# Storing h as hi and lo parts, loading them from GpSimd's queue, and S5 and linear attention without GpSimd arithmetic

## Chip, cores and metric

The kernel runs on one core of a Trainium2 chip. The metric is the device time of one execution in microseconds (us). An engine is called by its name in the profile: PE (TensorE matmuls), DVE (VectorE), ACT (ScalarE), POOL (GpSimd) and SP (SyncE, which begins most transfers).

## What is computed

One decoder layer on 2048 tokens of width 1024. A modulated RMSNorm gives h; one projection of h feeds three token mixers (gated linear attention, sparse attention over the best 256 keys, and the S5 state-space layer), whose outputs are joined by one projection; a mixture of 32 experts follows. Cut to what the change touches:

```
h = rms_norm(x, norm1_g) * (1 + sc1) + sh1
proj = h @ w_in                       # 2616 columns, split among the mixers
g = log_sigmoid(lr @ gate_w + gate_b) / GLA_TAU          # gates of linear attention
bcum = cumsum(g); q_dec = q * exp(bcum); k * exp(-bcum); k * exp(blast - bcum)
o = rms_norm(o, norm_g) * silu(r)                         # linear attention
_, _, h_re, h_im = associative_scan(combine, (a_re_t, a_im_t, x_re, x_im))   # S5
score = where(admissible, score, -inf); _, sel = top_k(score, 256)           # sparse attention
```

## The kernel before

h is kept in fp32 precision by writing each operand of a product as hi + lo, both rounded to a 32-bit form that PE multiplies faster; a product is then three matmuls (`mm3`, lines 162 to 164). Weights are split in `load_split` (ACT makes hi in line 176, DVE or POOL the rest in line 177).

**Sweep 1** (`prep`, `tok1`, `scores`, lines 308 to 411) goes over the tokens in 8 chunks of 256. It builds h transposed (`ht`), splits it into `xh` (DVE, line 333) and `xl` (POOL, line 334), stores `ht` to `hT_d` in DRAM by a transfer of SP (line 335), and projects the columns for the indexer and for `u`; the indexer's scores are accumulated on DVE (line 255).

**The later sweeps** (`sweep2`, line 445) need h again for the other columns: 2a (the `v` and `r` columns, 410 to 547 us in the profile), 2b (`gqk_d`, to about 684 us), 2c (the rest of `r` and `dv_d`, to about 775 us) and, later, DQ (`dqk_d`, about 1045 to 1245 us). Each has 8 chunks; for each chunk `load_h` (line 431) brings two tiles `xr` of 512 KB by SP (line 437), ACT makes hi from each (line 440) and POOL lo (line 441). `load_h` for the next chunk stands at the start of a chunk.

Between 420 and 775 us the sweeps are woven with the choice of the 256 keys: ten rounds of counting (`select`), in which ACT counts one part of the keys (line 805) and DVE another (line 808), then DVE joins the counts in some fifteen instructions of 14 numbers each (lines 812 to 836). DVE also computes the parameters of S5 (`params`) and the gates' sums (`gates`, lines 549 to 555, with a subtraction on POOL in line 552). `masks` (from line 844) follows: a penalty per block of keys (line 858 on DVE, line 859 on DVE or POOL) and a mask.

**S5 and linear attention** (775 to 1045 us): `s5_tables` (line 909) builds power tables for 6 groups at a time, three instructions per table, by `powers` (lines 929 to 934); `TGI` says which of the four tables POOL builds (0, 2 and 3; DVE builds the fourth). `s5_states` (line 1168) and `s5_outputs` (line 1202) use them, and linear attention (`gla_prep`, `gla_block`, `gla_tail`) is woven in; its last part runs beside DQ. At about 819 us all engines meet at a branch on a flag (line 1013).

A scheduler orders each engine's instructions when the program is built, from dependences and an own estimate of times; so a change in one place moves instructions in others. Each engine takes its instructions in that order, and a transfer on a queue waits behind those before it.

The instruction of line 441 that much of the prediction speaks of is this:

```
S.activation(xx[0][-1], xr, AF.Copy)
G.tensor_sub(xx[1][-1], xr, xx[0][-1].bitcast(F32))
```

Of the kernel before, what the change touches and what calls it, by code (L numbers as in the profile page):

```python
# [9 lines left out]
F32 = mybir.dt.float32  # L10
# [4 lines left out]
AF = mybir.ActivationFunctionType  # L15
# [5 lines left out]
P = 128  # L21
# [19 lines left out]
def body(tc, x, c, ada_w, ada_b, norm1_g, w_in, gla_gate_w, gla_gate_b, gla_norm_g, dsa_norm_g,  # L41
# [97 lines left out]


    C1 = 256
    hT_d = dr.tile([KD, P, T], F32, name="hT_d")
    u_d = dr.tile([T, 384], F32, name="u_d")
    v_d = dr.tile([T, 384], F32, name="v_d")
    r_d = dr.tile([T, 384], F32, name="r_d")
# [162 lines left out]
    def prep(ch):  # L308
# [16 lines left out]
        for k0 in range(0, KD, 4):  # L325
            ht = s1.tile([P, KD * P], F32, name="ht", tag="ht").rearrange("p (k c) -> p k c", c=C1)
            for k in range(k0, k0 + 4):
                pt = s1p.tile([P, 2, C1], F32, name="pt", tag="pt", bufs=2)[:, 0]
                for i in range(2):
                    TE.transpose(pt[:, i * P:(i + 1) * P], xs[i][:, k * P:(k + 1) * P], ident)  # L330
                S.activation(ht[:, k - k0], pt, AF.Identity, scale=gain[:, k:k + 1], bias=modc[:, 0, k:k + 1])
                yield
            V.tensor_copy(xh[:, k0:k0 + 4], ht)
            G.tensor_sub(xl[:, k0:k0 + 4], ht, xh[:, k0:k0 + 4].bitcast(F32))
            nc.sync.dma_start(hT_d[k0:k0 + 4, :, t0:t0 + C1].rearrange("k p t -> p k t"), ht)
        iqs = ts_.tile([P, 8, C1], F32R, name="iqs", bufs=2)
        st_[ch] = (xh, xl, iqs)
        for m in (2, 0, 1):
# [87 lines left out]

    SWA = 12
    SCO = list(range(2, NB))
    WB, PPB, PJB, XRB, XXB = 3, 3, 3, 4, 3

    def load_h(ch):

        t0 = ch * C1
        xx = [[], []]
        for k0 in range(0, KD, 4):
            xr = fp.tile([P, 4, C1], F32, name="xr", tag="xr", bufs=XRB)
            nc.sync.dma_start(xr, hT_d[k0:k0 + 4, :, t0:t0 + C1].rearrange("k p t -> p k t"))
            for j in range(2):
                xx[j].append(fp.tile([P, 4, C1], F32R, name=f"xx{j}", bufs=XXB))
            S.activation(xx[0][-1], xr, AF.Copy)  # L440
            G.tensor_sub(xx[1][-1], xr, xx[0][-1].bitcast(F32))  # L441
        return xx
    xx_ = {}

    def sweep2(job, last=False):
# [23 lines left out]
        for ch in range(T // C1):  # L469
            t0 = ch * C1  # L470
            xx = xx_.pop(ch)
            nx = (ch + 1) % (T // C1)
            if nx or not last:
                xx_[nx] = load_h(nx)
            if feat:
                ft = fp.tile([P, 4, C1], F32, name="ft", tag="xr", bufs=4)

                pps = [fpp.tile([P, 2, C1], F32, name="pp", bufs=PPB) for m in range(2)]
                for z in range(2):
                    for m in range(4):  # L480
                        for k in range(z * 4, z * 4 + 4):
                            mm3(pps[m // 2][:, m % 2], [w[:, k, m * P:(m + 1) * P] for w in w2],
                                (xx[0][z][:, k % 4], xx[1][z][:, k % 4]), k, KD - 1, -1 if m % 2 else 0,
                                skip_group_check=True)
                        if m % 2:
                            if z:
                                S.activation(ft[:, m - 1:m + 1], pps[m // 2], AF.Copy)  # L487
                            yield
                nc.sync.dma_start(job[1][:, :, t0:t0 + C1].rearrange("m p t -> p m t"), ft)
            else:  # L490
                N = sum(n for _, n, _, _ in job)
                pjs = [fpp.tile([P, 512], F32, name="pj", bufs=PJB)[:, :N] for i in range(2)]
                for z in range(2):
                    for i in range(2):
                        cs = slice(i * P, (i + 1) * P)
                        for k in range(z * 4, z * 4 + 4):
                            mm3(pjs[i], (xx[0][z][:, k % 4, cs], xx[1][z][:, k % 4, cs]),
                                (w2[0][:, k, :N], w2[1][:, k, :N]), k, KD - 1)
                        if z:
                            tok_store(job, ch * 2 + i, fp, pjs[i])  # L500
                        yield
# [18 lines left out]
    def gates():  # L520
        with tc.tile_pool(name="gg", bufs=1, side="right") as gg, \
# [15 lines left out]
            for t0 in range(0, T, H2):  # L537
                lr = gg.tile([16, H2], F32, name="lr")
                nc.sync.dma_start(lr, lr_d[:, t0:t0 + H2])
                for p_ in range(2):  # L540
                    ta = gg.tile([P, H2], F32, name="ta")
                    tm = gg.tile([P, H2], F32, name="tm")
                    for c0 in range(0, H2, CH):
                        cs = slice(c0, c0 + CH)
                        pg = ggp.tile([P, CH], F32, name="pg")
                        TE.matmul(pg, wg[:, 2 * p_:2 * p_ + 2].rearrange("r h d -> r (h d)"), lr[:, cs], start=True,
                                  stop=True)
                        S.activation(ta[:, cs], pg, AF.Abs, bias=gb2[:, p_:p_ + 1])
                        V.tensor_scalar(tm[:, cs], pg, gb2[:, p_:p_ + 1], 0.0, op0=OP.add, op1=OP.min)
                    S.activation(ta, ta, AF.Exp, scale=-1.0)  # L550
                    S.activation(ta, ta, AF.Ln, bias=1.0)
                    G.tensor_sub(tm, tm, ta)
                    for c0 in range(0, H2, CH):
                        cs = slice(c0, c0 + CH)
                        V.tensor_tensor_scan(ta[:, cs], rst, tm[:, cs], 0.0, op0=OP.mult, op1=OP.add)
                    nc.sync.dma_start(bc_d[p_, :, t0:t0 + H2], ta)
                    yield
# [338 lines left out]
    pnx = ExitStack()  # L896
    pn = pnx.enter_context(tc.tile_pool(name="pn", bufs=2, side="right"))
    MSK = [(masks(list(z), a_, i, pn), 2 * len(z)) for i, (z, a_, e, _) in enumerate(SELS)]
    RJ, TGI = (), (0, 2, 3)
    SPT, SPU, SPY, TGT, TGY = 1, 2, 1, 't', 'y'  # L900
    s5x = ExitStack()
    s5 = s5x.enter_context(tc.tile_pool(name="s5", bufs=2))
# [162 lines left out]
    def gla_prep(ch):  # L1065
# [13 lines left out]
        S.activation(o.enb, o.enb, AF.Exp, scale=-1.0 / 16.0)  # L1079
        o.qd, o.ki = o.gq[:, 0:2], o.gq[:, 2:4]  # L1080
        V.scalar_tensor_tensor(o.qd, o.qd, 48.0 ** -0.5, o.eb, op0=OP.mult, op1=OP.mult)
        G.tensor_mul(o.ki, o.ki, o.enb)
        G.tensor_mul(o.kd.rearrange("p m (n c) -> p m n c", c=64), o.ki.rearrange("p m (n c) -> p m n c", c=64),
                     o.eb[:, :, 63::64][:, :, :, None].to_broadcast([P, 2, 4, 64]))
        o.og = ga.tile([P, 2, 384], F32, name="og")
        o.ss = ga.tile([P, 2, 4], F32, name="ss")
# [2 lines left out]
    def gla_block(o, i):  # L1089
# [35 lines left out]
        sq = ga.tile([P, 384], F32, name="sq")  # L1125
        S.activation(sq, o.og[:, i], AF.Square)
        V.tensor_reduce(o.ss[:, i], sq.rearrange("p (h c) -> p h c", h=4), op=OP.add, axis=AX)
        G.tensor_mul(o.rt[:, i], o.rt[:, i], o.og[:, i])

    def gla_tail(o, ch):  # L1130
        t0 = ch * C1
# [32 lines left out]
    with tc.tile_pool(name="s5s", bufs=2) as s5s:  # L1164
# [3 lines left out]
        def s5_states(t):  # L1168
# [14 lines left out]
            for n in range(NS_):  # L1183
# [3 lines left out]
                V.tensor_mul(xa[:, n], px[:, 0], ct[:, g0 + n])  # L1187
                V.tensor_mul(xb[:, n], px[:, 1], st[:, g0 + n])
                yield
            G.tensor_add(xa, xa, xb)  # L1190
            for n in range(NS_):
                gg = gb * GB + g0 + n
                V.tensor_tensor_scan(gt[:, n], prm[:, 4, gg:gg + 1].to_broadcast([P, NCK]), xa[:, n], 0.0,
                                     op0=OP.mult, op1=OP.add)
            yield
            V.memset(p1[:, :, :, 0:1], 0.0)
            G.tensor_mul(p1[:, 0, :, 1:], gt[:, :, :NCK - 1], ct[:, ss_, :NCK - 1])
            V.scalar_tensor_tensor(p1[:, 1, :, 1:], gt[:, :, :NCK - 1], -1.0, st[:, ss_, :NCK - 1], op0=OP.mult,
                                   op1=OP.mult)
            yield  # L1200
# [970 lines left out]
```

## Time and profile before

| What | us |
|---|---|
| Runs: median of 3 (lowest to highest) | 2953.65 (2953.2 to 2962.46) |
| The profiled execution's own time | 2958.35 |
| Its span | 2956.3 |
| Mean granted clock of PE (share of full) | 0.883 |
| PE busy | 2390.8 (81%) |
| DVE busy | 2105.1 (71%) |
| ACT busy | 1345.6 (46%) |
| POOL busy | 1032.1 (35%) |

The profile is one execution; times in it are counted from its span's start. Busy time is summed per engine; what an engine waited for is inferred from its semaphores. Shares over the whole span say little here, since the stages have different limits; the stages named above are read one by one.

### The profile page before, as it was taken

How to read it: one execution, taken by the hardware profiler on the slowest of the kernel's cores; microseconds unless marked ns; L12 is line 12 of the kernel's file. 1: busy time of each engine (PE TensorE's matmuls, PEld its weight loads, DVE VectorE, ACT ScalarE, POOL GpSimd, SP SyncE). 2: the span in 40 equal slices, each digit the busy share in tenths (PEclk: the TensorE clock that was granted, in tenths of full speed). 3: DMA queues.
4: the chain of work that ended last, by engine and by line, in shares of the span. 5: the costliest groups of instructions: out<-in, count | busy, mean ns of one | idle time of the engine just before them, and what ended most of it. 6: DMA issues, size and time to landing. Idle time of an engine off the chain costs nothing. (4 is left out here: it accounts for less than half of the span.)

```text
span 2956.3 us, 38623 instructions
## 1 busy us (share of the span) xinstructions
PE 2390.8 (81%) x12563; PEld 1866.4 (63%) x12563; DVE 2105.1 (71%) x4742; ACT 1345.6 (46%) x2337; POOL 1032.1 (35%) x765
## 2 busy tenths in 40 slices
PE   4989877777568899948897999488877988889995
PEld 3766645776546767736675778476655566656673
DVE  6478867999988864547787565677766777667774
ACT  2568867574122244446665222155433444444442
POOL 2221133436645332155543345304322333222321
PEclk9999967888776879958998899688988999989998
DMA  7222254433331244244322543397777888778882
GB/s 217 86 92 85 80 201 155 113 136 124 107 114 46 71 153 126 84 140 121 100 80 86 174 143 130 91 288 212 250 225 228 261 269 262 243 252 267 277 259 82
DMA packets 372280, 474.93 MB, mean 161 GB/s; under 512 B 85924, under 2 KB 272452, under 8 KB 371814
## 3 DMA queue, kind: packets, MB, share of 16 engines
q1 hardware_dynamic: 334501, 421.83, 44.6%
q0 software_dynamic: 37568, 50.56, 6.2%
q8 instruction: 100, 1.64, 0.2%
q14 instruction: 111, 0.90, 0.1%
HBM read 385.75 MB, written 112.23 MB: 168 GB/s over the span
## 5 line engine op out<-in xcount | busy, mean ns | idle before, releaser
L1921 DVE TENSOR_TENSOR wl<-wraw,wh 128x1024 fp32r<-128x1024 f32 x272 | 329.1, 1220 | 162.5 <-ACT wh L1920 156.3
L1920 ACT ACTIVATE wh<-wraw 128x1024 fp32r<-128x1024 f32 x272 | 286.2, 1054 | 296.7 <-PE pd L164 107.8
L1970 PE MATMUL pg<-xT,wh 128*128 128x352 f32 (+10 forms) x1152 | 325.4, 362 | 12.0 <-DVE xT L1902 6.7
L1944 PE MATMUL pg<-wraw,xT 128*120 128x512 f32 (+9 forms) x448 | 225.0, 663 | 82.0 <-DVE ga__21999 L1977 12.9
L1972 PE MATMUL pg<-xT,wl 128*128 128x176 f32 (+10 forms) x1152 | 283.7, 246 | 1.5 <-DVE wl L1921 1.5
L441 POOL TENSOR_TENSOR xx<-xr,xx 128x1024 fp32r<-128x1024 f32 x64 | 162.9, 2546 | 273.2 <-ACT xx L440 261.1
L1970 PEld LDWEIGHTS pg<-xT,wh 128*128 128x128 f32 x1152 | 224.1, 195 | 17.2 <-DVE xT L1902 7.9
L1972 PEld LDWEIGHTS pg<-xT,wl 128*128 128x128 f32 x1152 | 227.3, 197 | 2.5 <-DVE wl L1921 2.0
L1944 PEld LDWEIGHTS pg<-wraw,xT 128*120 128x120 f32 (+9 forms) x448 | 85.8, 196 | 212.3 <-issue 115.5
L255 DVE SCALAR_TENSOR_TENSOR sb<-rl,iws,sb 128x1024 f32<-128x1024 f32 (+7 forms) x154 | 186.6, 1211 | 33.3 <-ACT rl L254 24.9
L2018 POOL DMA_INDIRECT yp_d<-y,ix x50 | 94.4, 1887 | 311.0 <-DVE y L2015 173.5
L162 PE MATMUL pd<-wh,hid 128*104 128x512 f32 (+17 forms) x400 | 163.5, 409 | 23.8 <-ACT hid L1954 12.3
L162 PE MATMUL pp<-xx,w 128*128 128x256 f32 x512 | 155.1, 303 | 20.1 <-ACT ft L487 10.0
L254 ACT ACTIVATE rl<-pi,iwa 128x1024 f32<-128x1024 f32 (+7 forms) x176 | 157.2, 910 | 30.5 <-DVE sb L255 25.9
L163 PE MATMUL pd<-wl,hid 128*104 128x512 f32 (+17 forms) x400 | 159.5, 399 | 0.0
L164 PE MATMUL pd<-wh,hid 128*104 128x512 f32 (+17 forms) x400 | 158.7, 402 | 0.0
L163 PE MATMUL pp<-xx,w 128*128 128x256 f32 x512 | 152.7, 299 | 3.1 <-POOL xx L441 3.1
L164 PE MATMUL pp<-xx,w 128*128 128x256 f32 x512 | 152.0, 298 | 2.0 <-DVE w L177 1.2
L251 PE MATMUL pi<-iks,iqs 128*128 128x512 f32 (+3 forms) x304 | 110.9, 448 | 32.1 <-ACT rl L254 31.2
L162 PE MATMUL pj<-w,xx 128*128 128x512 f32 (+1 forms) x256 | 100.2, 393 | 40.7 <-DVE ot L208 19.2
L1538 DVE CUSTOM_DVE_ANT_0 pr<-ps,mk 128x512 f32<-128x512 f32 (+3 forms) x160 | 94.2, 605 | 49.9 <-PE ps L1537 28.2
L2005 POOL DMA_INDIRECT part<-yp_d,ix x50 | 68.6, 1373 | 163.2 <-DMA yp_d<-y,ix 154.2
(1076 smaller groups left out, 6975.9 us busy)
## 6 DMA issues: line engine op xcount, KB each, us to landing
wraw<-in_exp_w_gate_dram SPq DMA_DIRECT2D x128, 512.0 KB
wraw<-in_exp_w_up_dram SPq DMA_DIRECT2D x128, 512.0 KB
wraw<-in_exp_w_down_dram SPq DMA_DIRECT2D x128, 512.0 KB
xr<-hT_d SPq DMA_DIRECT2D x64, 512.0 KB
w<-in_ada_w_dram SPq DMA_DIRECT2D x64, 256.0 KB
w<-in_ada_w_dram SPq DMA_DIRECT2D x16, 512.0 KB
xi<-in_x_dram SPq DMA_DIRECT2D x16, 512.0 KB
hT_d<-ht SPq DMA_DIRECT2D x16, 512.0 KB
```

What stands on the lines that cost most here:

```text
L162: TE.matmul(ps, st[0], mv[0], start=(k == first), stop=False, **kw)
L163: TE.matmul(ps, st[0], mv[1], start=False, stop=False, **kw)
L164: TE.matmul(ps, st[1], mv[0], start=False, stop=(k == last), **kw)
L251: TE.matmul(pi[:, s0:s0 + sl], iqs[:, h, i * P:(i + 1) * P], iks[:, g0 + s0:g0 + s0 + sl], start=True, stop=True)
L254: S.activation(rl[:, :gl], pi[:, :gl], AF.Relu, scale=iwa[:, b, h:h + 1])
L255: V.scalar_tensor_tensor(sb[:, gs], rl[:, :gl], iws[:, b, h:h + 1], (eps if h == 0 else sb)[:, gs], op0=OP.mult, op1=OP.add)
L441: G.tensor_sub(xx[1][-1], xr, xx[0][-1].bitcast(F32))
L1920: S.activation(wh, w, AF.Copy)
L1921: V.tensor_sub(wl, w, wh.bitcast(F32))
L1944: TE.matmul(pgs[a][:C], xT[:, kk], wp[2 * i + a][:, k], start=(kk == 0), stop=(kk == KD - 1))
L1970: TE.matmul(pgs[m], wh[:, k, ws], xT[:, i * 4 + k], start=(i + k == 0), stop=False, skip_group_check=True)
L1972: TE.matmul(pgs[m][:, 0], wl[:, k, ws], xT[:, i * 4 + k, 0], start=False, stop=(i + k == 4), skip_group_check=True)
```

## The change

Sweep 1 stores `xh` and `xl` instead of `ht`, in two DRAM arrays `hx_d`, so two transfers of SP for each half chunk instead of one. In `load_h` each half chunk is now two transfers of 512 KB, begun by POOL (`G.dma_start`), straight into the tiles `xx`, and the copy on ACT and the subtraction on POOL are gone. There are four tiles of each kind instead of three, and no `xr`. Seven pieces of arithmetic move from POOL to DVE: the gates' subtraction, three tables of S5 (`TGI` is empty), two products in `gla_prep`, one in `gla_block`, one sum and one product in `s5_states`. The subtractions of weights (line 177 and 468) and of the penalties (line 859) stay on POOL in part.

```diff
-    hT_d = dr.tile([KD, P, T], F32, name="hT_d")
+    hx_d = [dr.tile([KD, P, T], F32, name=f"hx{j}_d") for j in range(2)]
...
-            nc.sync.dma_start(hT_d[k0:k0 + 4, :, t0:t0 + C1].rearrange("k p t -> p k t"), ht)
+            for z_d, z in zip(hx_d, (xh, xl)):
+                nc.sync.dma_start(z_d[k0:k0 + 4, :, t0:t0 + C1].rearrange("k p t -> p k t"), z[:, k0:k0 + 4].bitcast(F32))
...
-    WB, PPB, PJB, XRB, XXB = 3, 3, 3, 4, 3
+    WB, PPB, PJB, XXB = 3, 3, 3, 4
...
-            xr = fp.tile([P, 4, C1], F32, name="xr", tag="xr", bufs=XRB)
-            nc.sync.dma_start(xr, hT_d[k0:k0 + 4, :, t0:t0 + C1].rearrange("k p t -> p k t"))
             for j in range(2):
                 xx[j].append(fp.tile([P, 4, C1], F32R, name=f"xx{j}", bufs=XXB))
-            S.activation(xx[0][-1], xr, AF.Copy)
-            G.tensor_sub(xx[1][-1], xr, xx[0][-1].bitcast(F32))
+                G.dma_start(xx[j][-1], hx_d[j][k0:k0 + 4, :, t0:t0 + C1].rearrange("k p t -> p k t"))
...
-                    G.tensor_sub(tm, tm, ta)
+                    V.tensor_sub(tm, tm, ta)
...
-    RJ, TGI = (), (0, 2, 3)
+    RJ, TGI = (), ()
...
-        G.tensor_mul(o.ki, o.ki, o.enb)
-        G.tensor_mul(o.kd.rearrange("p m (n c) -> p m n c", c=64), o.ki.rearrange("p m (n c) -> p m n c", c=64),
+        V.tensor_mul(o.ki, o.ki, o.enb)
+        V.tensor_mul(o.kd.rearrange("p m (n c) -> p m n c", c=64), o.ki.rearrange("p m (n c) -> p m n c", c=64),
...
-        G.tensor_mul(o.rt[:, i], o.rt[:, i], o.og[:, i])
+        V.tensor_mul(o.rt[:, i], o.rt[:, i], o.og[:, i])
...
-            G.tensor_add(xa, xa, xb)
+            V.tensor_add(xa, xa, xb)
...
-            G.tensor_mul(p1[:, 0, :, 1:], gt[:, :, :NCK - 1], ct[:, ss_, :NCK - 1])
+            V.tensor_mul(p1[:, 0, :, 1:], gt[:, :, :NCK - 1], ct[:, ss_, :NCK - 1])
```

How the order moves, at three places (the changed kernel's lines from 144 on are shifted by one or two). First SP's queue at the start of sweep 1, where `wstage` is the first weight of the sweep's second product, `xi` a row block of x, `lr_d` a small store and `dcol` a parameter. Before:

```order
L726 DMA dcol<-in_s_d_dram 16x24x1 x3
L335 DMA hT_d<-ht 128x4x256
L287 DMA xi<-in_x_dram 128x1024
L335 DMA hT_d<-ht 128x4x256
L174 DMA wstage<-in_w_in_dram 128x2x384
```

and in the changed kernel:

```order
L725 DMA dcol<-in_s_d_dram 16x24x1 x5
L337 DMA hx_d<-xh 128x4x256
L337 DMA hx_d<-xl 128x4x256
L337 DMA hx_d<-xh 128x4x256
L337 DMA hx_d<-xl 128x4x256
L367 DMA lr_d<-lr 16x256
L175 DMA wstage<-in_w_in_dram 128x2x384
```

The first weight now stands behind four stores, two of which wait for POOL, and behind the store of `lr_d`. Next POOL's queue at the end of 2b and in 2c, where `pen` is the penalty. Before:

```order
L441 TENSOR_TENSOR xx_5567<-xr,xx_5566 128x1024
L859 TENSOR_TENSOR pen<-pen,scr_3401 128x384
L441 TENSOR_TENSOR xx_5573<-xr,xx_5572 128x1024
L859 TENSOR_TENSOR pen<-pen,scr_3403 128x640
L441 TENSOR_TENSOR xx_5641<-xr,xx_5640 128x1024
```

and in the changed kernel:

```order
L858 TENSOR_TENSOR pen<-pen,scr_3418 128x384
L440 DMA xx_5387<-hx_d 128x4x256
L440 DMA xx_5385<-hx_d 128x4x256
L858 TENSOR_TENSOR pen<-pen,scr_3420 128x640
L858 TENSOR_TENSOR pen<-pen,scr_3422 128x896
L440 DMA xx_5515<-hx_d 128x4x256
L440 DMA xx_5513<-hx_d 128x4x256
L858 TENSOR_TENSOR pen<-pen,scr_3424 128x1152
L440 DMA xx_5519<-hx_d 128x4x256
L178 TENSOR_TENSOR w_5492<-wstage,w_5491 128x2x384
```

Transfers now stand where the subtractions stood, and the penalties come earlier than the weights of 2c. Last DVE's queue at the first tables (`va`, `vb`, `za`, `zb` with helpers `t4v`; `ct` and `st` are rotations). Before:

```order
L932 TENSOR_TENSOR vb<-bb_3696,pbr 128x768
L933 TENSOR_TENSOR t4v<-bb_3697,par 128x768
L948 MEMSET ct 128x6
L949 MEMSET st 128x6
L934 TENSOR_TENSOR vb<-vb,t4v 128x768
```

and in the changed kernel:

```order
L931 TENSOR_TENSOR va<-bb_3697,par 128x768
L932 TENSOR_TENSOR t4v<-bb_3698,pbr 128x768
L931 TENSOR_TENSOR vb<-bb_3697,pbr 128x768
L933 TENSOR_TENSOR va<-va,t4v 128x768
L931 TENSOR_TENSOR za<-cx_3695,pa 128x768
L932 TENSOR_TENSOR t4v<-bb_3698,par 128x768
L931 TENSOR_TENSOR zb<-cx_3696,pa 128x768
L933 TENSOR_TENSOR vb<-vb,t4v 128x768
```

All four tables are now in DVE's own order, nine instructions more for each set of six groups.

## Rows read from the trace of the kernel before

**Rows 1.** Busy time per stretch: us, each engine (instructions), granted clock, DMA share, GB/s.
```profile
420.00:775.00 355.00, 279.76 (x1536) 250.75 (x1534) 294.11 (x650) 205.82 (x351) 153.89 (x67) 0.87 0.43 142
775.00:1045.00 270.00, 187.59 (x943) 148.98 (x944) 230.52 (x531) 57.25 (x118) 133.93 (x103) 0.71 0.28 84
1045.00:1245.00 200.00, 190.40 (x1158) 153.76 (x1158) 103.14 (x240) 84.43 (x166) 52.79 (x27) 0.93 0.37 119
...
690.00:775.00 85.00, 69.30 (x366) 67.04 (x364) 77.95 (x132) 24.45 (x46) 50.20 (x18) 0.92 0.35 113
```

**Rows 2.** Waits, 420 to 775 us: engine, line, waited for, us, times, longest.
```profile
DVE cnt L812 <- ACT j L805: 21.9, 5, 14.4
DVE ta L555 <- POOL tm L552: 13.3, 3, 6.7
...
PE pj L162 <- DVE ot L208: 19.2, 4, 9.2
```

**Rows 3.** Timeline, POOL and DVE around 650 us: start, us, instruction.
```profile
649.38 2.38 POOL L441 TENSOR_TENSOR xx<-xr,xx 128x1024 fp32r<-128x1024 f32 x1 [14.46 <-ACT xx L440]
...
649.84 1.96 DVE L832 SCALAR_TENSOR_TENSOR f<-cl,w 128x14 f32<-128x14 f32 x1
651.83 0.17 DVE L833 TENSOR_SCALAR f<-f 128x14 f32<-128x14 f32 x1
```

**Rows 4.** Timeline, a count on DVE and a subtraction on POOL at one time.
```profile
599.62 2.20 DVE L808 TENSOR_SCALAR_CACHE_REDUCE j<-scr,t 128x1920 bf16<-128x1920 f32 x1
...
600.45 2.39 POOL L441 TENSOR_TENSOR xx<-xr,xx 128x1024 fp32r<-128x1024 f32 x1 [2.90 <-ACT xx L440]
```

**Rows 5.** Timeline, DVE: first and last held instruction, 420 to 775 and 775 to 1045 us.
```profile
440.58 1.00 DVE L812 SCALAR_TENSOR_TENSOR cnt<-cnt,nkh 128x9 f32<-128x9 f32 x1 [14.42 <-ACT j L805]
...
760.50 2.40 DVE L873 SCALAR_TENSOR_TENSOR j<-iota,f,tops 128x8 f32<-128x8 f32 x1
...
778.74 2.32 DVE L932 TENSOR_TENSOR vb<-bb,pbr 128x768 f32<-128x768 f32 x1
...
1037.44 1.59 DVE L1137 TENSOR_TENSOR rt<-rt,rs_y 128x384 f32<-128x384 f32 x1
```

**Rows 6.** Groups of instructions by line: count, busy us, mean ns, idle before.
```profile
L440 ACT ACTIVATE xx<-xr 128x1024 fp32r<-128x1024 f32 x64 | 67.4, 1054 | 47.9 <-issue 24.9 <-PE pj L163 14.1 <-PE pp L164 5.4
...
L932 DVE TENSOR_TENSOR vb<-bb,pbr 128x768 f32<-128x768 f32 x2 | 1.9, 944 | 0.0
...
L1197 POOL TENSOR_TENSOR p<-gt,ct 128x510 f32<-128x510 f32 x12 | 19.0, 1582 | 21.8 <-DVE gt L1193 11.9 <-DVE rs_t L64 3.9 <-DVE tmp L959 3.1
L1128 POOL TENSOR_TENSOR rt<-rt,og 128x384 f32<-128x384 f32 x9 | 10.2, 1131 | 31.4 <-ACT og L1124 31.4
L1082 POOL TENSOR_TENSOR gq<-gq,enb 128x512 f32<-128x512 f32 x6 | 8.7, 1453 | 29.3 <-ACT enb L1079 26.9 <-DMA gq<-gqk_d 2.4
```

**Rows 7.** Waits, DVE from 820 and PE from 775 to 1045 us.
```profile
DVE gt L1193 <- POOL xa L1190: 6.6, 4, 3.6
...
PE pm L983 <- DVE kt L976: 41.1, 4, 21.6
```

**Rows 8.** Transfers begun by POOL: one line (min/median/max ns), one instruction of the timeline.
```profile
L2018 POOL DMA_INDIRECT yp_d<-y,ix x50: 936/1406/4924, 1988.3 to 2938.6; - x50
...
2007.30 4.43 POOL L2031 DMA_INDIRECT out_dram<-part,ix  x1 [0.30 <-issue]
```

**Rows 9.** Loads of h in 2b: SP's timeline, and the stretch in which four moved.
```profile
643.21 8.95 SPq L437 DMA_DIRECT2D xr<-hT_d  x4
...
643.50:650.00 6.50, 6.50 (x52) 6.50 (x52) 5.56 (x16) 5.71 (x9) 0.62 (x1) 0.91 0.97 314
```

**Rows 10.** Timeline at the start of sweep 1: POOL and SP.
```profile
54.17 2.37 POOL L334 TENSOR_TENSOR xl<-ht,xh 128x1024 fp32r<-128x1024 f32 x1 [0.63 <-DVE xh L333]
...
53.77 1.99 SPq L174 DMA_DIRECT2D wstage<-in_w_in_dram  x2
...
60.43 0.34 SPq L365 DMA_DIRECT2D lr_d<-lr  x1
```

More of the change, by code (lines that the diff above doesn't have):

```diff
@@ L475, in sweep2 @@
             if feat:
-                ft = fp.tile([P, 4, C1], F32, name="ft", tag="xr", bufs=4)
+                ft = fp.tile([P, 4, C1], F32, name="ft", bufs=2)
                 pps = [fpp.tile([P, 2, C1], F32, name="pp", bufs=PPB) for m in range(2)]
```

## The prediction, on record before the changed kernel ran

> **What bounds the kernel now.** I read the table of stretches first, since the shares over the whole span mix stages. The profiled execution has an own time of 2958.35 us (span 2956.3); the median of the runs is 2953.65. The sum below is made against 2958.35, and 4.7 us are taken off at the end.
>
> In the woven sweeps, 420 to 775 us, DVE is busy for 294.1 of 355 us and PE for 279.8 at a granted clock of 0.87 [rows 1]. DVE sets the pace: PE's named wait there is for a copy of DVE [rows 2]. From 775 to 1045 us it is DVE again, 230.5 of 270, with PE at 187.6; in DQ, 1045 to 1245, PE is busy for 190.4 of 200 and bounds alone [rows 1].
>
> Next, what DVE's busy time is made of. At 649.84 us an instruction on 14 numbers, L832, takes 1.96 us and ends at 651.80; its twin in size, L833, takes 0.17. POOL's subtraction of L441 ran from 649.38 to 651.76 [rows 3]: the small instruction stood until POOL was done. Not every DVE instruction is held: a count of 1920 columns with one tensor as input (L808, 2.20 us) runs through a whole L441 [rows 4]. So most of what the sweeps lose to POOL is hidden inside busy DVE rows, not in waits.
>
> I took a clean price for each DVE instruction: 0.17 us at 14 numbers a partition [rows 3] and 0.944 at 768 [rows 6] give 0.16 us and 1.02 ns per number. Held are those that overlap arithmetic of POOL and last over 0.15 us more than that. From 420 to 775 us these are 40, from the one at 440.58 to the one at 760.50, and their excess adds up to 63.7 us, 47.9 of it behind L441. From 775 to 1045 they are 58, from 778.74 to 1037.44, with 65.0 us, all behind operations that now leave POOL [rows 5]. In DQ 18 more hold 23.1 us, but DVE has room there.
>
> **The change part by part.**
>
> *Sweeps 2a to 2c: -50.* DVE's 294.1 loses the 47.9 behind L441 and gains four subtractions of the gates, 1024 numbers at 1.21 us by the clean price, 4.8: 251. DVE idled for 355 - 294 = 61 us; the 21.9 behind ACT's counts stay, and of the 13.3 behind the gates' subtraction about 7 go (three times POOL's 2.4; the rest of that wait is for ACT ahead of it) [rows 2]. That leaves 54, and 251 + 54 = 305 us instead of 355. PE's 279.8 still fits, without much room. The 64 copies on ACT (1.05 us each, 67.4 in all [rows 6]) go as well; ACT waits for others more than they wait for it, so I credit nothing. If the waits behind ACT shrank with them, up to 22 more would go.
>
> *The transfers.* 128 transfers begun by POOL replace 64 of SP: per chunk four of 512 KB instead of two. Four of the old kind moved at 314 GB/s, DMA share 0.97 [rows 9]; 2 MB then need 6.7 us. The shortest chunks, those of 2c, last 85 / 8 = 10.6 us at a DMA share of 0.35 [rows 1], so the doubled load fits. No row shows a transfer that goes into the rounded type. At full rate it costs nothing; at half the rate a chunk needs 13.4 us, 2.8 more than it has, 22 us over 2c. I take nothing, since it is a plain move of the same 32 bits in size, and keep 22 for the range. Eight buffers of 512 KB hold two chunks, so a load may be a chunk early.
>
> *The issue on POOL.* No row shows a plain transfer begun by POOL. The nearest are its gathers: 0.94 to 4.92 us, median 1.4 [rows 8]. At 1.4 a chunk costs POOL 5.6 us, hidden under 10.6 or more; L441, at 2.4 each two a chunk, cost it nearly as much. I take nothing for it; at the long end it decides (rival A). What stands against it is that an issue may be slowed by DVE: the gather of 4.43 us at 2007 us waited for nothing that the profile shows [rows 8]. The Trainium skill ("SBUF — State Buffer", section "SBUF: two separate sides") has a rule for that: GpSimd makes the descriptors of its own transfers, and is locked out while DVE holds the port pair that they share; it advises a queue of SP or ACT. By that rule each issue would last until DVE's instruction ends, and the sum would go to rival A where such holds add up; by the median gather it stays as above. The rows bear out that DVE and POOL exclude each other, but not how long descriptors wait.
>
> *POOL's queue.* In 2b and 2c the transfers now stand between penalties and subtractions of weights. A penalty on POOL waits for DVE, and a transfer behind it waits too; a transfer that waits for PE to free a tile holds up the weights behind it. With a chunk's lead I cost it at nothing; rival B is that it isn't hidden.
>
> *S5 and linear attention: -8.* DVE's 230.5 loses 65.0 [rows 5]. It gains three tables of three instructions for four sets, 36 at 0.95 (768 numbers, L932 [rows 6]): 34.2. The sum and the product of `s5_states`, 12 each at 0.68 (L1197 took POOL 1.58 [rows 6]): 16.3. Linear attention's two products, six each at 0.68 (L1082 [rows 6]): 8.2. The nine of L1128 at 0.55: 5.0. Together 63.7, so DVE is busy for 229.2. Of its 39.5 us of waits the 6.6 for POOL's sum [rows 7] go: 262 us instead of 270. What was saved in held time is thus spent on the work itself; between both ends lie +20 (rival C) and -20, if the waits of PE behind DVE shorten too.
>
> *DQ: -3.* PE can lose at most 200 - 190.4 = 9.6 us of waits [rows 1]; I take a third.
>
> *Sweep 1: -1.* At its end, 345 to 420 us, the same sum of excess gives 5.6 us behind L441 of the first loads: -5. At the start SP's queue now has the first weight (53.77 us [rows 10]) behind two stores of `xl`, ready at 54.17 + 2.37 = 56.5, and behind `lr_d`, which was issued at 60.43 [rows 10]: the weight comes up to 6.7 us later. PE has the other product's matmuls to do meanwhile, so I take +4, between 0 and 6.7. The 16 added stores move 8 MB over 420 us in which the queues are mostly free.
>
> Sum: -50 - 8 - 3 - 1 = -62; 2958.35 - 62 = 2896, and 4.7 less for the median: **2892 us**.
>
> **The rivals.**
>
> *A, POOL can't begin the transfers fast enough (slower).* From 2a to 2c there are 24 chunks of four: 96 issues of c us. POOL keeps about 28 us of other arithmetic there: its 153.9 [rows 1] less 45 of L441 (116) and four subtractions of the gates (9.5). With the other terms worth -12, the kernel is slower once 96c + 28 exceeds 355 + 12: c over 3.5 us. At the 4.43 of the long gather [rows 8] the stretch takes 453 us, +98, less 12: +86, about 3040 us. For it: such gathers exist, and DVE is busier than where they ran. Against: the median is 1.4, and a DVE instruction in the sweeps lasts 0.45 us on average (294.1 for 650 [rows 1]). Chance 0.09.
>
> *B, the queue of POOL couples the sweeps to DVE.* Transfers late behind penalties, or weights late behind transfers, make PE wait; half of the 50 comes back: 2917 us. For it: 2a to 2c have PE at 279.8 of what would be 305, little slack to catch up, and a load now needs POOL free, where SP's queue did nothing but wait. Against: a chunk of lead. Chance 0.17.
>
> *C, the added arithmetic of S5 lies on the path.* PE waits for 41.1 us for `kt` of DVE [rows 7]; if the 63.7 us of new instructions come where PE waits for DVE, and the held ones came where nobody did, the stretch grows by 20 instead of shrinking by 8: 2920 us. Chance 0.13.
>
> That the change does nothing, because the held time only moves to ACT's waits, would need ACT to bound the sweeps; it is busy for 205.8 of 355 us [rows 1]. I count it with B.
>
> **How the numbers follow.** My forecast has 0.61, A 0.09, B 0.17, C 0.13. The range goes from 2850 (22 more behind ACT, 10 in DQ instead of 3, -20 in S5: -103 in all, 2850 on the scale of the median) to 2938, which takes in B, C and most of both together. What remains outside is A, B with half-rate transfers, and a little below. About 0.3%, 9 us, is what a measurement can tell from no change. Slower than that is A with most of its chance, 0.08; within it, 0.07, lie a mild A, and B with C and the 22 us of slow transfers; the rest, 0.85, is faster.
>
> **What would show it.** Right: the stretch of the woven sweeps falls from 355 to about 305 us with DVE busy for about 251; the joins of counts (L812 to L836) take 0.17 to 0.3 us each; ACT's L440 and POOL's L441 are gone, and the rows of POOL's transfers show issues of 1 to 2 us; S5 lasts about 262 us with DVE's share unchanged; DQ lasts about 197. Wrong: PE waiting for the transfers into `xx`, POOL's issues at 3 us or more or PE waiting for weights behind them (A, B); longer waits of PE for `kt`, or the first table's end later (C). It would also be wrong if the held time of DVE didn't vanish with L441, because transfers that POOL begins hold DVE as its arithmetic did.

## The result and the profile after

The changed kernel takes 2918.57 us (median of 4 runs, 2912.58 to 2927.89) against 2955.61 (median of 4): a ratio of 0.9867 with a 95% interval of 0.983 to 0.9903, 37 us faster. The forecast was 2892 us, 64 less than that median, in a range from 2850 to 2938. The profiled execution took 2917.04 us, 41.3 less than the one of before.

To see where they went I cut both executions at the same events of the program: the first matmul of 2a, the last of 2c, the last that feeds S5's states (`px`), the first of attention, the first of the experts. The stretches of the kernel before, with the columns of [rows 1]:

```profile
0.00:410.40 410.40, 316.24 (x1576) 235.97 (x1576) 307.19 (x469) 261.64 (x436) 83.92 (x106) 0.92 0.36 116
410.40:773.90 363.50, 289.33 (x1565) 258.46 (x1565) 298.86 (x678) 209.01 (x355) 154.09 (x67) 0.87 0.43 141
773.90:1012.80 238.90, 158.80 (x797) 126.36 (x797) 210.73 (x469) 48.29 (x99) 123.52 (x96) 0.71 0.26 79
1012.80:1278.60 265.80, 230.36 (x1352) 183.57 (x1351) 140.31 (x357) 105.61 (x208) 73.47 (x45) 0.87 0.38 120
1278.60:1917.60 639.00, 521.50 (x2881) 426.04 (x2881) 431.37 (x1421) 273.63 (x529) 304.61 (x257) 0.88 0.37 118
1917.60:2956.30 1038.70, 874.61 (x4396) 636.03 (x4396) 716.60 (x1352) 447.38 (x711) 292.50 (x196) 0.92 0.77 241
```

and those of the changed kernel:

```profile
0.00:408.90 408.90, 319.23 (x1577) 238.75 (x1577) 299.75 (x469) 259.45 (x433) 80.28 (x111) 0.92 0.44 138
408.90:749.10 340.20, 278.56 (x1565) 249.85 (x1565) 266.39 (x701) 167.74 (x310) 95.28 (x127) 0.88 0.88 232
749.10:977.70 228.60, 172.97 (x797) 133.36 (x797) 189.95 (x520) 49.11 (x99) 0.00 (x0) 0.69 0.23 69
977.70:1228.30 250.60, 221.13 (x1351) 177.32 (x1350) 124.19 (x378) 90.81 (x192) 37.86 (x43) 0.91 0.58 161
1228.30:1863.60 635.30, 519.48 (x2880) 425.25 (x2880) 429.63 (x1421) 273.79 (x529) 304.40 (x257) 0.88 0.37 119
1863.60:2914.70 1051.10, 880.36 (x4396) 639.16 (x4396) 716.03 (x1352) 447.28 (x711) 282.83 (x196) 0.91 0.77 238
```

Line by line: sweep 1 -1.5 us, the woven sweeps -23.3 (forecast -50), S5 and DQ together -10.3 - 15.2 = -25.5 (forecast -8 - 3), attention and routing -3.7, the experts +12.4. In the sweeps DVE's busy time fell from 298.9 to 266.4, although four subtractions of the gates (4.9 us) and eight more masks (`mk`, 8.4 us) are in it: about 46 us of held time are gone, where 47.9 had been worked out. Those masks stood behind the sweeps before, so the border between sweeps and S5 has moved too; from the first matmul of 2a to the first of attention it is 819.4 us after 868.2, -48.8 for a forecast of -61. A join of the counts is now free of POOL, one row of many, with the columns of [rows 3]:

```profile
572.76 0.17 DVE L831 SCALAR_TENSOR_TENSOR f<-cl,w 128x14 f32<-128x14 f32 x1
573.02 0.17 DVE L832 TENSOR_SCALAR f<-f 128x14 f32<-128x14 f32 x1
```

So DVE got its time back, and the stretch shortened by half of the forecast only. What PE waits for in the changed kernel's sweeps (engine, line, waited for, us, times, longest) is partly new against [rows 2], the waits for transfers above all:

```profile
PE pj L163 <- DVE ot L209: 16.8, 3, 10.9
PE pp L163 <- ACT w L466: 7.2, 1, 7.2
PE pj L165 <- DMA xx<-hx_d: 7.2, 1, 7.2
PE pj L163 <- DMA xx<-hx_d: 7.0, 1, 7.0
...
PE pj L164 <- DVE w L178: 3.4, 1, 3.4
PE pj L164 <- POOL w L178: 1.9, 1, 1.9
```

For ACT it waits less: 20.4 us in all, after 41.6 in the kernel before, where no single line was as long as the 19.2 for DVE in [rows 2] but these add up to more:

```profile
PE pj L162 <- ACT ot L210: 11.8, 3, 7.5
PE pp L162 <- ACT ft L487: 10.0, 3, 6.4
PE pp L162 <- ACT w L467: 8.2, 1, 8.2
PE pj L162 <- ACT w L176: 8.1, 1, 8.1
```

By parts: 2a lasted 137.3 us after 138.8 before, 2b 112.9 after 133.8, 2c 90.0 after 90.8. Nearly the whole gain is in 2b. At the start of 2c PE stands, and the timeline of POOL and PE there (start, us, instruction, in brackets what ended the idle time before it) tells why:

```profile
658.17 2.09 POOL L858 TENSOR_TENSOR pen<-pen,scr 128x896 f32<-128x896 f32 x1 [2.61 <-DVE pen L857]
660.21 1.66 POOL L440 DMA_DIRECT2D xx<-hx_d  x2
663.82 2.60 POOL L858 TENSOR_TENSOR pen<-pen,scr 128x1152 f32<-128x1152 f32 x1 [1.96 <-DVE pen L857]
666.38 1.03 POOL L440 DMA_DIRECT2D xx<-hx_d  x1
667.43 1.81 POOL L178 TENSOR_TENSOR w<-wstage,w 128x768 fp32r<-128x768 f32 x1
...
666.68 0.69 PE L163 MATMUL pj<-w,xx 128*128 128x384 f32 x1 [7.02 <-DMA xx<-hx_d]
669.30 0.69 PE L164 MATMUL pj<-w,xx 128*128 128x384 f32 x1 [1.94 <-POOL w L178]
674.95 0.69 PE L164 MATMUL pj<-w,xx 128*128 128x384 f32 x1 [3.36 <-DVE w L178]
```

POOL waits for DVE before it can do a penalty; the transfers behind that penalty are begun at 660.21 only, their packets run from 662.25 to 666.25, and PE waits 7.02 us for them. The subtraction of a weight of 2c, whose hi part ACT had made at 658.99, runs at 667.43, behind two penalties and three transfers. That is rival B.

In S5 two waits of PE became shorter. For `kt`, which DVE makes from the first table, it waited 41.1 us before [rows 7], and for that table (`va`) itself

```profile
PE pvt L967 <- POOL va L934: 10.7, 1, 10.7
```

In the changed kernel no wait for POOL is left there, and the one for `kt` is

```profile
PE pm L982 <- DVE kt L975: 16.1, 4, 5.2
```

### The profile page after: what moved, and what is told of

Its sections match the earlier page's. It is cut to its first block, busy times and chain, and to the rows that moved or that the text cites. A ratio compares the mean times of both kernels' runs of the same rounds, so it can differ in the third digit from the quotient of the medians.

```text
span 2914.7 us, 38620 instructions
## 1 busy us (share of the span) xinstructions
PE 2391.7 (82%) x12563; PEld 1863.7 (64%) x12563; DVE 2026.0 (70%) x4838; ACT 1288.2 (44%) x2273; POOL 800.7 (27%) x733
## 5 line engine op out<-in xcount | busy, mean ns | idle before, releaser
L440 POOL DMA_DIRECT2D xx<-hx_d x128 | 98.0, 770 | 573.6 <-PE ptk L1141 242.5
L256 DVE SCALAR_TENSOR_TENSOR sb<-rl,iws,sb 128x1024 f32<-128x1024 f32 (+7 forms) x154 | 178.0, 1156 | 35.2 <-ACT rl L255 26.0
L2017 POOL DMA_INDIRECT yp_d<-y,ix x50 | 86.5, 1729 | 323.9 <-DVE y L2014 182.3
L163 PE MATMUL pp<-xx,w 128*128 128x256 f32 x512 | 152.5, 298 | 15.0 <-ACT w L466 7.2
L165 PE MATMUL pp<-xx,w 128*128 128x256 f32 x512 | 150.1, 294 | 5.5 <-DVE w L467 5.2
L164 PE MATMUL pp<-xx,w 128*128 128x256 f32 x512 | 149.0, 291 | 1.6 <-DMA xx<-hx_d 1.6
```

The costliest lines, as they stand in the source:

```text
L163: TE.matmul(ps, st[0], mv[0], start=(k == first), stop=False, **kw)
L164: TE.matmul(ps, st[0], mv[1], start=False, stop=False, **kw)
L165: TE.matmul(ps, st[1], mv[0], start=False, stop=(k == last), **kw)
L256: V.scalar_tensor_tensor(sb[:, gs], rl[:, :gl], iws[:, b, h:h + 1], (eps if h == 0 else sb)[:, gs], op0=OP.mult, op1=OP.add)
L440: G.dma_start(xx[j][-1], hx_d[j][k0:k0 + 4, :, t0:t0 + C1].rearrange("k p t -> p k t"))
```

## The experiments

Each run names what it changes against the kernel before or the changed kernel. "Start of attention" is the first of its matmuls, 1278.6 us before and 1228.3 in the changed kernel; up to there nearly all effects of the change are in, so I use it beside the totals.

**1. Only the storing and the loading** (changed kernel, the seven pieces of arithmetic back on POOL).

```diff
-    RJ, TGI = (), ()
+    RJ, TGI = (), (0, 2, 3)
-                    V.tensor_sub(tm, tm, ta)
+                    G.tensor_sub(tm, tm, ta)
...
```

> Only the storing and the loading of the two parts; the seven pieces of arithmetic stay on GpSimd. My theory (the sweeps gain because the subtraction after each load no longer holds VectorE, S5 gains from the moved arithmetic): the sweeps, from the first to the last matmul of 2a to 2c, last about 340 us as in the changed kernel (363.5 before), S5 and DQ together about 470 as before; total about 2930. Rival (S5 shortens because the last masks leave it, which the loads bring about): S5 and DQ shorten by 10 or more here too, total 2920 or below.

2942.84 us, ratio 0.9953 (0.9933 to 0.9973). The sweeps took 340.4 us, S5 and DQ 464.4 from the last matmul of 2c to the last of DQ (466.6 before). By stage this is my theory, and the rival falls; the total is 13 us above mine, and the experts' part is 11 us longer here than before (1049.8 after 1038.7). Start of attention 1250.4, 28.2 earlier than before. The run also has the change's other numbers of buffers: four of each `xx` instead of three, and two of `ft` (an output tile of 2b and DQ) where it shared four with `xr`. No run takes these apart.

**2. Only the seven moves** (kernel before, arithmetic moved, loads as they were).

```diff
-    RJ, TGI = (), (0, 2, 3)
+    RJ, TGI = (), ()
-            G.tensor_add(xa, xa, xb)
+            V.tensor_add(xa, xa, xb)
...
```

> Only the seven moves from GpSimd to VectorE; h is loaded and split as before. My theory: the sweeps stay within 358 to 364 us (the gates' subtraction is 4 of 150 operations), S5 and DQ shorten by 15 to 26 us; total about 2930 to 2938. Rival (the S5 gain hangs on the loads): S5 and DQ shorten by at most 10; total 2945 or above.

2931.29 us, ratio 0.9916 (0.9889 to 0.9943). The sweeps took 358.5 us, S5 and DQ 450.4, 16.1 less than before. Start of attention 1259.2, 19.4 earlier. The two halves add up: 28.2 + 19.4 = 47.6 of the change's 50.3, and 13.9 + 25.5 = 39.4 us of the medians for the change's 37.

**3. POOL's queue cleared** (changed kernel, penalties and the weights' subtractions of the sweeps on DVE).

```diff
-    GP = (2, 4, 6, 8, 10)
+    GP = ()
-            tok_weights(job, w2, fp, bufs=WB)
+            tok_weights(job, w2, fp, bufs=WB, eng=V)
...
```

> The changed kernel with all penalties and all subtractions of the sweeps' weights on VectorE, so that GpSimd's queue in the sweeps holds little but transfers. If the coupling through GpSimd's queue took the missing 25 us: 2c falls from 90 us to 75 to 80, although VectorE gets 5 penalties (5.4 us) and 8 weights (8 us) more; total about 2905. If the transfers' rate or VectorE bounds 2c: 2c stays at 88 to 95; total 2918 or above.

2913.32 us, ratio 0.985 (0.9819 to 0.9881). 2c fell from 90.0 to 78.0 us, the sweeps to 326.9, start of attention to 1219.4, though DVE does more. 2c is as the coupling had it; 2a stayed at 136.9. The total is 8 us above what I expected, and its interval overlaps that of the changed kernel, so the gain is shown by stage and not by the total.

**4. The same loads begun by SP** (changed kernel; both ends are also declared as plain 32-bit numbers, which run 6 takes apart).

```diff
-                G.dma_start(xx[j][-1], hx_d[j][k0:k0 + 4, :, t0:t0 + C1].rearrange("k p t -> p k t"))
+                nc.sync.dma_start(xx[j][-1].bitcast(F32), hx_d[j][k0:k0 + 4, :, t0:t0 + C1].rearrange("k p t -> p k t"))
```

> The changed kernel with the same loads begun by SyncE instead of GpSimd, both ends taken as plain 32-bit numbers. If the coupling through GpSimd's queue is the loss: the weights of 2c come 8 us earlier, 2c falls to 75 to 80 us, total about 2905. If the rate of the doubled transfers is the loss (7 us in 2a, 7 in 2c): 2a 130 and 2c 88 to 92 as in the changed kernel, total about 2918. If GpSimd's transfers are slower because they go into the rounded type, the DMA share at the same bytes falls here.

2895.86 us, ratio 0.9792 (0.9767 to 0.9817). 2a lasted 129.6 us, 2b 110.2, 2c 83.4 (between the two branches), the sweeps 323.2 (the row stands below, after run 6). Six masks fall behind the sweeps again; start of attention 1216.2, 12.1 earlier than in the changed kernel. What is left at the start of 2c is again a queue, POOL's with the penalties alone. PE's wait there:

```profile
PE pj L164 <- POOL w L178: 13.5, 1, 13.5
```

and what POOL does meanwhile, by the timeline:

```profile
653.88 3.79 POOL L858 TENSOR_TENSOR pen<-pen,scr 128x1408 f32<-128x1408 f32 x1 [5.01 <-DVE pen L857]
657.63 5.10 POOL L178 TENSOR_TENSOR w<-wstage,w 128x768 fp32r<-128x768 f32 x2
```

**5. SP's loads, and the penalties on DVE.**

```diff
-    GP = (2, 4, 6, 8, 10)
+    GP = ()
```

> Loads begun by SyncE, and all penalties on VectorE; the subtractions of weights stay where they were. If the 13.5 us that TensorE waits for a weight's subtraction at the start of 2c (in the run with SyncE's loads) come from that subtraction standing behind penalties in GpSimd's queue: the wait goes, 2c falls from 83 to about 70 to 75 us, total about 2885. If VectorE (5.4 us more of penalties) or the weights' own transfers bound it: 2c stays at 80 or above, total 2893 or above.

2890.9 us, ratio 0.9778 (0.9753 to 0.9802). The wait is gone and 2c takes 72.3 us. This beats the kernel before and the changed one; its interval overlaps that of run 4. The sweeps, whole, and 2c:

```profile
407.20:719.30 312.10, 273.60 (x1565) 245.97 (x1565) 249.68 (x687) 169.52 (x310) 15.27 (x13) 0.91 0.74 243
...
647.00:719.30 72.30, 69.19 (x384) 67.91 (x384) 47.07 (x111) 13.83 (x35) 4.00 (x2) 0.98 0.79 256
```

DVE is busy for 249.7 us here, and the sweeps last 363.5 - 312.1 = 51.4 us less than before, with as many masks in them: near the -50 and the 251 of the forecast. That both agree so well is partly luck, since the five moved penalties cost DVE 5.4 us that the forecast didn't have, and free it of being held beside them: the five penalties that DVE did next to POOL's took 15.0 us in run 4 and take 6.1 here. So the run isn't a measure of the queue alone. Start of attention 1205.9, 22.4 earlier than in the changed kernel.

**6. POOL's loads without the rounded type** (changed kernel).

```diff
-                G.dma_start(xx[j][-1], hx_d[j][k0:k0 + 4, :, t0:t0 + C1].rearrange("k p t -> p k t"))
+                G.dma_start(xx[j][-1].bitcast(F32), hx_d[j][k0:k0 + 4, :, t0:t0 + C1].rearrange("k p t -> p k t"))
```

> The changed kernel with GpSimd's transfers declared as plain 32-bit numbers at both ends, as in the run with SyncE. Packets of 1024 bytes took a median of 61 ns in GpSimd's queue and 46 in SyncE's. If the rounded type costs it: 46 ns here, the stall of 7 us in 2a and part of 2c go, total about 2905. If GpSimd's queue costs it: 61 ns again, total about 2918.

2921.94 us, ratio 0.9852 (0.9823 to 0.9882). Neither branch as I wrote it. The rounded type does cost transfer time: without it the packets became 4096 bytes with a median of 159 ns, 40 per KB instead of 61, and the DMA share of the sweeps fell from 0.88 to 0.70. But the sweeps last as long. The sweeps in this run:

```profile
412.10:755.90 343.80, 277.00 (x1565) 248.91 (x1565) 264.55 (x701) 168.08 (x310) 94.63 (x127) 0.88 0.70 230
```

and with SP's loads (run 4):

```profile
406.90:730.10 323.20, 274.66 (x1565) 247.57 (x1565) 255.56 (x683) 169.51 (x310) 28.86 (x18) 0.89 0.72 235
```

The same bytes, the same plain type, nearly the same DMA share, and 20.6 us between them. (The profiled execution of run 6 was its slowest, 2936.6 us; between the medians lie 26 us.) The rate of the transfers isn't what was lost; the queue that begins them is (with the order that the scheduler then makes of the rest, which is not the same in both).

**7. The issuing alone** (run 4, and beside each load a transfer of 512 pieces of 4 bytes on POOL's queue).

```diff
+                G.dma_start(dz[j][:, :, 0:1], hx_d[j][k0:k0 + 4, :, t0:t0 + 1].rearrange("k p t -> p k t"))
```

> Loads begun by SyncE, and beside each a tiny transfer of 512 pieces of 4 bytes begun by GpSimd (128 in all): the issuing without the bytes. If beginning transfers on GpSimd holds VectorE as its arithmetic does: small VectorE instructions beside the issues take 0.7 us more, 30 to 60 us in the sweeps, total 2915 or above. If issues are harmless: total 2893 to 2900. The experts' part, with the same instructions in all kernels, lasted 1038 us with SyncE's loads and 1050 to 1057 with GpSimd's; if it is GpSimd's issuing that lengthens it, it is above 1045 here, total about 2910.

2970.18 us, ratio 1.0047 (1.003 to 1.0065). Slower, but not for the reason that I had: the tiny transfers write the same two small tiles again and again and so wait for each other's landing (123.0 us in the sweeps), and a weight's subtraction stood behind them. POOL's timeline, the last two rows before it and itself:

```profile
595.36 1.48 POOL L442 DMA_DIRECT2D dz<-hx_d  x2 [1.06 <-DMA dz<-hx_d]
597.88 1.52 POOL L442 DMA_DIRECT2D dz<-hx_d  x2 [1.04 <-DMA dz<-hx_d]
599.42 1.81 POOL L469 TENSOR_TENSOR w<-wz,w 128x768 fp32r<-128x768 f32 x1
```

and PE's wait for it:

```profile
PE pp L165 <- POOL w L469: 59.1, 2, 57.5
```

So the run is no measure of harmless issues by its total. What it does show: the issue itself takes 0.75 us, and 57.5 us of waiting of PE can hang on one subtraction behind transfers. Does an issue hold DVE? Yes, but little. In the changed kernel's sweeps 49 DVE instructions of 14 numbers overlap one and last 203 ns on average, 506 at most; the 139 others 173. Four of those that last longest, 0.42 to 0.51 us, end within 0.03 us of the issue's end, as this one at 418.11:

```profile
416.62 1.49 POOL L440 DMA_DIRECT2D xx<-hx_d  x2 [31.88 <-PE pj L165]
...
417.67 0.44 DVE L799 TENSOR_SCALAR nt<-t 128x14 f32<-128x14 f32 x1
```

DVE holds an issue in the same way. Of the changed kernel's 128 issues seven last over 0.9 us, and six of these end 0.30 us after a comparison on DVE with one tensor as input (L857, L885). Two of them, 2.19 us together instead of 1.5:

```profile
721.58 0.69 DVE L885 TENSOR_SCALAR mk<-scr,ntau 128x896 bf16<-128x896 f32 x1 [2.35 <-DMA mask_d<-mk]
722.65 0.75 DVE L885 TENSOR_SCALAR mk<-scr,ntau 128x1024 bf16<-128x1024 f32 x1 [0.39 <-DMA mask_d<-mk]
...
721.52 2.19 POOL L440 DMA_DIRECT2D xx<-hx_d  x2 [2.36 <-PE pj L165]
```

All six together lose 2.3 us by it. The experts' part lasted 1043.6 us in run 7, below the 1045 that I had set as a sign of GpSimd's issuing.

**8. Three tables back on POOL** (run 4).

```diff
-    RJ, TGI = (), ()
+    RJ, TGI = (), (0, 2, 3)
```

> Loads begun by SyncE, three of the four power tables back on GpSimd; the other moved arithmetic stays on VectorE. My theory (the tables' long run on GpSimd holds VectorE's small rotations, lines 955 to 960, and that is most of what S5 gained): S5 and DQ together get 12 to 20 us longer (448 in the run with SyncE's loads), with the rotations back at 100 to 118 us of busy time instead of 68; total about 2912. Rival (the gain came from linear attention and the sum and product of the states, whose results TensorE waits for): S5 and DQ longer by at most 5, total about 2900.

2912.96 us, ratio 0.9848 (0.9825 to 0.9871), 17 us slower than run 4. S5 and DQ took 466.9 instead of 447.9 us. One of the six lines of rotations, a group with its count, busy time, mean and idle time, here:

```profile
L956 DVE TENSOR_TENSOR ct<-ct,tmp 128x6 f32<-128x6 f32 (+7 forms) x32 | 21.5, 671 | 0.0
```

and in run 4:

```profile
L956 DVE TENSOR_TENSOR ct<-ct,tmp 128x6 f32<-128x6 f32 (+7 forms) x32 | 11.3, 353 | 0.0
```

All six lines together took 109.7 us instead of 67.6. PE's wait for `kt`, which DVE makes from the first table, is back with them, 50.8 us instead of 16.2:

```profile
PE pm L982 <- DVE kt L975: 50.8, 4, 21.8
```

My theory holds: the tables on POOL held rotations on DVE.

**9. The subtraction after each load on DVE, nothing else** (kernel before).

```diff
-            G.tensor_sub(xx[1][-1], xr, xx[0][-1].bitcast(F32))
+            V.tensor_sub(xx[1][-1], xr, xx[0][-1].bitcast(F32))
```

> The kernel before with the subtraction after each load on VectorE instead of GpSimd, and nothing else changed. By the held time of my working VectorE loses 48 us of it in the sweeps and gains 45 subtractions of 1.21 us, 54: busy for about 300 instead of 294, the sweeps 365 to 375 us instead of 363.5; total 2957 to 2970. If VectorE was not held (its busy time is its own): busy for about 350, the sweeps 400 us or more, total 2990 or above.

2946.04 us, ratio 0.9954 (0.9933 to 0.9974): faster, though DVE takes on 45 subtractions in the sweeps. That stretch:

```profile
407.10:736.60 329.50, 275.64 (x1565) 247.24 (x1565) 282.25 (x646) 206.00 (x353) 40.53 (x22) 0.91 0.47 152
```

and the group of the moved subtractions in it:

```profile
L441 DVE TENSOR_TENSOR xx<-xr,xx 128x1024 fp32r<-128x1024 f32 x45 | 58.8, 1311 | 27.3 <-ACT xx L440 27.3
```

VectorE's held time was real and paid for the work. The 282.25 us by themselves don't show it, since the 14 masks all fall behind the sweeps here; from the first matmul of 2a to attention, with 61 of the subtractions in it, DVE is busy for 651.93 us, as the third number below has it, after 649.9 before:

```profile
407.10:1259.50 852.40, 665.85 (x3712) 558.14 (x3712) 651.93 (x1563) 361.08 (x660) 193.89 (x147) 0.83 0.38 120
```

The rival (its busy time is its own) would need over 720. My numbers were off too: the sweeps' matmuls end after 329.5 us, not 365, but the masks end 2.5 us earlier only (815.7 after 818.2), so much of it comes back in S5. Start of attention 1259.5, 19.1 earlier.

**10. One more subtraction on POOL per half chunk** (changed kernel).

```diff
+            G.tensor_sub(dz[1], dz[0], dz[0])
```

> The changed kernel with one more subtraction of 128x1024 numbers on GpSimd for each half chunk, of constant tiles, whose result nobody reads (64 in all). My theory: VectorE is held again by 35 to 50 us in the sweeps, and they last 355 to 370 us instead of 340; total about 2940. Rival (the sweeps gained by ACT's copies and by the split itself being gone, not by held time): the sweeps stay at 338 to 346 us, total 2918 to 2925.

3023.05 us, ratio 1.0211 (1.0187 to 1.0236), 104 us slower than the changed kernel. That is far beyond my 2940, and the size says little: with nothing to wait for, the 64 ran crowded between 374 and 557 us, not spread over four sweeps. The hold itself is plain there. DVE's sum of scores at the end of sweep 1 in this run:

```profile
L256 DVE SCALAR_TENSOR_TENSOR sb<-rl,iws,sb 128x1024 f32<-128x1024 f32 (+1 forms) x8 | 22.1, 2766 | 0.6
```

and in the changed kernel:

```profile
L256 DVE SCALAR_TENSOR_TENSOR sb<-rl,iws,sb 128x1024 f32<-128x1024 f32 (+1 forms) x17 | 23.4, 1376 | 3.0 <-ACT rl L255 1.6
```

**11. One more copy on ACT per half chunk** (changed kernel).

```diff
+            S.activation(dz[1], dz[0], AF.Copy)
```

> The changed kernel with one more copy of 128x1024 numbers on ScalarE for each half chunk, of a constant tile, whose result nobody reads (64 in all, 1.05 us each). My theory (ScalarE has room in the sweeps, what it gave back was not the gain): the sweeps stay at 338 to 350 us, 2b at 112 to 118; total 2918 to 2930. Rival (the copies that went were what 2b gained): 2b back to 125 us or more, total 2935 or above.

2961.46 us, ratio 0.9998 (0.9983 to 1.0012), 43 us slower than the changed kernel: the whole gain. The total is the rival's, but the mechanism is neither's: the sweeps' matmuls took 321.6 us, 18.6 less than in the changed kernel, and 2b 119.6, between both. What came late is the choice of the keys. The rounds of counting, in which DVE waits for ACT's part, ended at 677.3 us instead of 648.7, all 14 masks fell behind the sweeps and ended at 825.4 instead of 744.3, and PE then waited for the flag that is made with them:

```profile
PE pf L1009 <- DVE fail L884: 41.9, 1, 41.9
```

The copies ran between 374 and 573 us, denser than those of the kernel before, so 43 is too much for what the change took off ACT. Copies so placed are not free, since they delay the counts; how much of the change's gain came from the copies that went stays open. PE's waits for ACT don't tell: in the sweeps they are about 20 us here, with copies added, and in run 9, which keeps the old ones, as in the changed kernel (20.4). And since the sweeps can shorten while the choice of the keys gets late, their length alone is a poor measure; the start of attention, 1272.7 here, shows the loss.

**12. The stores of sweep 1 begun by POOL** (run 5).

```diff
-                nc.sync.dma_start(z_d[k0:k0 + 4, :, t0:t0 + C1].rearrange("k p t -> p k t"), z[:, k0:k0 + 4].bitcast(F32))
+                G.dma_start(z_d[k0:k0 + 4, :, t0:t0 + C1].rearrange("k p t -> p k t"), z[:, k0:k0 + 4].bitcast(F32))
```

> As the run with SyncE's loads and all penalties on VectorE, with the stores of the parts in sweep 1 begun by GpSimd instead of SyncE. If the weights of sweep 1's second product were late because they stood behind those stores: the first of its matmuls comes at 66 us instead of 70.5, sweep 1 ends 2 to 4 us earlier. If its product waits for other things: no gain. Total 2887 to 2891, unless the 32 transfers that GpSimd begins lengthen the experts' part by 10 us as the runs with its loads suggest: then about 2898.

2898.93 us, ratio 0.9771 (0.9738 to 0.9805), no gain over run 5. The first matmul of sweep 1's second product came at 60.7 us instead of 71.4, yet its last at 361.0 instead of 359.8: the late weight of the start is covered by other matmuls. The experts' part took 1054.0 us, 11.3 more than in run 5, and the total is the one that I had given for that case.

## Why the prediction was right, and where it missed

- **Direction and range**: right. 2918.57 lies in the range, but beside rival B's 2917 (chance 0.17) and 27 us above my own figure (0.61). That the total came so near to B's is partly luck: the sweeps gave 26.7 us less than forecast and the experts took 12.4 more, while S5 and DQ gave 14.5 more and attention with the routing 3.7.
- **Held time in the sweeps (-47.9 of DVE)**: right. About 46 us went. Run 9 shows the cause by itself: 61 subtractions more on DVE, and its busy time up to attention stays the same.
- **A reading of the held time**: the count at 599.62 did not run through a whole L441; it ended at 601.82, L441 at 602.84 [rows 4]. That counts aren't held is right all the same: one of 1792 columns, begun at 656.46 while the L441 of 655.02 to 657.43 ran, took 2.08 us.
- **The sweeps (-50)**: wrong by 27. Eight masks, 8.4 us of DVE, ran in them instead of behind, so the loss is less than that; up to attention 12 us are missing (-48.8 for -61). The step that failed is "With a chunk's lead I cost it at nothing", on POOL's queue. The lead did not cover the queue: at the end of 2b POOL waited for DVE before each penalty, and transfers and weights of 2c stood behind. Clearing the queue gave 12 us in 2c (run 3), taking the loads off it 17 in all sweeps (run 4, 340.2 to 323.2), and clearing the penalties as well brought -51.4 (run 5); by the start of attention runs 4 and 5 are 12.1 and 22.4 us earlier. Rival B named this mechanism and half the gain. I had read the order of the queue and not followed one chunk through it.
- **The copies on ACT (0)**: open. My reason, that ACT waits for others more than they wait for it, leaves out that PE waited 41.6 us for ACT in the sweeps; I had read its longest line only, 19.2 us for DVE [rows 2]. The 41.6 fell to 20.4, but to about 20 in runs 9 and 11 too, which have copies. DVE's wait for ACT's counts fell from 21.9 to 15.9 us only. Run 11 shows that copies beside the counts can cost.
- **The issue on POOL**: right. 128 issues took 742 to 1555 ns, median 750, less than the 1.4 us that I took from the gathers, so rival A could not come. The Trainium skill ("SBUF — State Buffer", section "SBUF: two separate sides") says that GpSimd can't write descriptors while DVE runs an instruction in a mode that takes the port pair that both share. The trace agrees: six issues ended 0.30 us after a comparison on DVE, at a cost of 2.3 us in all (run 7). The page's advice, a queue of SP or ACT, was right here by run 4, but because of what stands in POOL's queue.
- **The rate of the transfers (0, up to +22)**: 0 was right. The rounded type does cost (61 ns per KB instead of 40), but run 6 shows that it wasn't on the path.
- **S5 and DQ (-11)**: too small, -25.5. The balance of held time against added work on DVE was right in kind: from the end of 2c to attention its busy time went from 351.0 to 314.1 us, 11.0 of it the eight masks that now end in the sweeps. What I didn't count are waits of PE. The one for `kt`, 41.1 us before [rows 7], is 16.1 now, so rival C's wait became shorter, and one of 10.7 for a table of POOL is gone. Run 2 gives 16 us without the loads, run 8 takes 19 back with the tables.
- **Sweep 1 (-1)**: -1.5, by luck. The first weight's transfer was issued at 60.44, 6.7 later than before, as worked out, but run 12 shows that nothing hung on it, so the +4 wasn't there and the -5 at the end came to less.
- **The experts (0)**: +12.4 in the profiled executions, by the same instructions with the same waits. In the profiles of runs without transfers of h by POOL this part took 1035 to 1045 us, with one of 1053 (run 9), in those with them 1044 to 1058. The granted clock there was 0.91 after 0.92, but run 4 has 0.91 too and took 1038.3. Whether it is chance stays open.

## What to carry to other kernels

When two engines hold each other, the loss is inside busy rows: compare the same small instruction beside and away from the other engine's arithmetic, and sum the excess by stretch. Before comparing two stretches, count what moved across their border. Before a queue gets transfers, follow the instructions that stand ahead of each one and what they wait for; a queue whose other work waits for a busy engine is a bad place for loads, however short an issue is. And a gain that is worked out for one engine holds only if the engine fed by it has no wait of its own next; write down what is late next for each part of the stretch.

## What the runs showed of the hardware

- A multiplication with a sum of mostly 1024 numbers on DVE, with two tensors as inputs, took 1.38 us on average in the changed kernel and 2.77 beside POOL's subtractions in run 10; a rotation of 6 to 768 numbers 353 ns on average without, and 671 with tables on POOL (run 8).
- A transfer of 512 KB begun by POOL took it a median of 0.75 us. Such an issue held small DVE instructions until it ended (0.42 to 0.51 us instead of 0.17), and a comparison on DVE with one tensor as input held it: six of 128 issues ended 0.30 us after one.
- A packet of 1024 bytes into the rounded type took a median of 61 ns; as plain numbers SP's took 46, and POOL's, in packets of 4096 bytes, 159.
